# Later modulation products, four row buffers and GpSimd stores in a fused state-space and attention trunk

## The chip, the cores and the metric

The kernel runs on one core of a Trainium2 chip. A core has five engines that run side by side, each in the order of its own queue: TensorE (PE, matmuls), VectorE (DVE), ScalarE (ACT), GpSimd (POOL) and SyncE (SP, which here only issues transfers). Transfers (DMAs) between the chip's memory and the on-chip SBUF are issued from the queues of SP, ACT and POOL. The metric is the device time of one execution in microseconds, lower is better; a time is the median of several runs.

## The reference, cut to what matters

Two layers work on x, 1024 tokens of 1024 channels. Every sub-layer is modulated by a vector c:

```python
m = silu(c) @ w + b                     # shift, scale, gate: 64 columns of 128 in all
h = rms(x, g) * (1 + scale) + shift

# layer 0: state-space mixer
u, z = split(h @ w_in)
y = gelu(scan(u) + D * u)
y = y * sigmoid(y @ w_glu + b_glu)      # "GLU"
y = y * silu(z)
x = x + gate * (y @ w_out)              # "output projection"

# shared keys, values, forget gates; layer 1: attention with decay
h = rms(x, kv_g) * (1 + scale) + shift
k, v, f = split(h @ kv_w)               # k with a norm per head
h = rms(x, b_g) * (1 + scale) + shift
q, z = split(h @ w_in)                  # q with a norm per head
o = attention(q, k, v, cumsum(log_sigmoid(f)))
x = x + gate * ((o * silu(z)) @ w_out)
```

The modulation `silu(c) @ w` has 64 outputs per partition. Each needs one tile of 128 x 1024 weights (512 KB) and one dot product of its rows with silu(c).

## The kernel before, in words

x is kept transposed, channels on partitions, in eight strips of 128 channels by 1024 tokens. Every matmul that must be precise is made of three: both operands are split into a high and a low half (`split`, lines 99 to 101; `split_part`, line 705) and the three larger products are added in PSUM.

The work runs in stages: preparation and the in-projection, the scan with the rest of the in-projection, the GLU (lines 742 to 762), the output projection (lines 773 to 804), the norm for the shared keys and values (lines 818 to 825), six token-wise jobs called v0, v2, k0, k2, q0 and q2 (lines 918 to 952), attention with the z strips of layer 1 between its steps, and the last projection.

The instructions are not run in the order in which the code gives them. A planner simulates the five engines and, on each, takes what is ready by then, earlier code first; a transfer or an instruction whose inputs are expected early can be drawn far ahead of its place. `tc.issue_after(i)` only says that what is issued in its block stays behind instruction `i` on that engine. On the chip each engine then runs its list strictly in order, and waits at an instruction whose inputs are not there.

Modulation: 16 of the 64 rows (shift and scale of layer 0) are handled at the start. `modulate(n0, n1)` (lines 135 to 139) treats the other 48: a buffer of the pool `mwp`, which has two, a load from SP's queue, and `gemv` (line 131), one DVE instruction that multiplies by silu(c) and sums. The GLU calls it for three rows in each of five slots (line 755), the output projection for one row in nine slots (line 784), the token jobs for two rows at twelve places in v0, v2 and k0 (line 941).

A GLU slot (e, i) is one strip e of output channels and one half i of the tokens. It loads z (line 750, two buffers) and, at i = 0, y (line 752); scales z (line 756), takes its sigmoid (line 757) and forms silu (line 758); projects (line 759), takes the sigmoid of the result (line 760), and multiplies both into y (lines 761 and 762). The first two projections, `psg`, are made before the slots begin. Projections have two PSUM buffers (`pj`).

An output slot (e, i) loads x (line 780), projects (line 785), adds the gated result to x (`L786`), stores the new x row to `x1_d` (line 788) for the last stage, and squares it (line 790). GpSimd adds the squares up (line 794); two matmuls with a constant matrix (lines 800 and 801) turn the sum into the mean square over all channels, and `neg2_rsqrt` into the inverse root. The new x is then scaled in place by it, strips in turn on DVE and GpSimd (line 824), and `modulated` makes the split operands `aH` and `aL` of the token jobs (lines 165 to 167).

A token job takes 2 x 256 columns of weights (`wide`, line 829, one raw buffer of 1 MB) and makes sixteen tiles of 128 tokens by 256 columns (`token_tile`, three PSUM buffers). A V tile is split (lines 862 and 863, `vt`, two buffers) and stored (line 866). A K or Q tile has a norm per head (lines 874 to 879: square on ACT, sum on DVE, two small steps on GpSimd, product `hnt` on DVE), four of them are turned on PE and stored (line 894).

At job q0 the pools of x1 and of modulation are closed, and the attention's tiles (`at0`) take over their memory as its last readers finish.

## Time and profile before

| | |
|---|---|
| Median of 3 runs | 1225.57 us (1224.21 to 1227.58) |
| The profiled execution's own time | 1223.69 us |
| Its span, first to last instruction | 1221.9 us |
| Mean granted TensorE clock | 0.987 |
| PE busy | 1162.0 us, 95% of the span |
| DVE, ACT, POOL busy | 848.9, 605.1, 367.8 us |
| GLU and output projection | about 299 to 495 us |
| Token jobs | about 487 to 820 us |
| Attention and last stage | about 820 to 1222 us |

In a row of a group or a timeline, `L132` is line 132 of the kernel, `out<-in` are tile names, and what stands in brackets is the idle time of the engine before the instruction and what ended it. `SPq` and `POOLq` are the issuing queues. A row of waits gives who waited for whom, the time in all, how often and the longest. Times within the span count from its start.

### The profile page before, as it was taken

The numbers are of one execution on the slowest core, as the hardware profiler recorded it, in microseconds if no ns is written. First come the engines' busy times: TensorE is split into PE (matmuls) and PEld (weight loads), VectorE is DVE, ScalarE is ACT, GpSimd is POOL, SyncE is SP. The second block draws the span as 40 slices with busy tenths as digits, with TensorE's granted clock in tenths as the row PEclk, the third lists the DMA queues.
The fourth block names the chain that finished last, engine by engine and source line by source line (L and its number), as shares of the span: only waits on it lengthen the run. The fifth ranks groups of instructions, "written<-read, shape, count | busy, mean of one in ns | idle before, by whom it ended". The sixth has DMA issues, their size and how long they took to land.

```text
span 1221.9 us, 20599 instructions
## 1 busy us (share of the span) xinstructions
PE 1162.0 (95%) x7542; PEld 1017.3 (83%) x7542; DVE 848.9 (69%) x1724; ACT 605.1 (50%) x1138; POOL 367.8 (30%) x568
## 2 busy tenths in 40 slices
PE   8989898997899998899989999999999999999898
PEld 6778887887778876799989989998888888888686
DVE  7889899874498767746444664448787778887421
ACT  6565766665335324322213452227677777886310
POOL 4000000000000033600133463447576666764100
PEclk9999999998989999999999999999999999999999
DMA  9754666584974885247543277518796968871242
GB/s 352 220 173 117 171 169 164 154 233 126 334 249 129 281 312 167 90 154 233 200 148 139 83 214 152 156 70 182 132 188 124 171 122 155 156 138 27 94 165 78
DMA packets 113333, 205.30 MB, mean 168 GB/s; under 512 B 17072, under 2 KB 58160, under 8 KB 111696
## 3 DMA queue, kind: packets, MB, share of 16 engines
q1 hardware_dynamic: 86272, 161.44, 41.4%
q0 software_dynamic: 24960, 37.75, 18.1%
q10 hardware_dynamic: 2000, 4.79, 1.7%
q8 instruction: 60, 0.98, 0.3%
q14 instruction: 41, 0.34, 0.1%
HBM read 146.47 MB, written 46.20 MB: 158 GB/s over the span
## 4 chain that ended last, share of the span: by engine, by line
PE 57%; DVE 16%; DMA 12%; ACT 5%; issue 5%; SPq 2%; POOL 2%; ACTq 0%; POOLq 0%; DVEq 0%
PE tkps L851 16%; PE zb L112 7%; PE pj_f L112 5%; PE tp L1043 5%; DMA modw<-modw 4%; PE u L264 4%; PE ov L1049 3%; PE ov L1050 3%; PE sp L1010 3%; DMA v_d<-vt 3%; PE sp L1011 3%; PE pj_g L112 2%; DMA mwx<-modw 2%; PE f L112 2%; DVE w_lo L101 1%
## 5 line engine op out<-in xcount | busy, mean ns | idle before, releaser
L851 PE MATMUL tkps<-wvh,aH 128*128 128x256 f32 (+1 forms) x768 | 220.5, 287 | 7.3 <-DVE vt L863 4.0
L851 PE MATMUL tkps<-wvh,aL 128*128 128x256 f32 (+1 forms) x768 | 217.1, 283 | 1.4 <-DVE aL L167 1.4
L851 PE MATMUL tkps<-wvl,aH 128*128 128x256 f32 (+1 forms) x768 | 216.7, 282 | 0.0
L851 PEld LDWEIGHTS tkps<-wvh,aH 128*128 128x128 f32 x768 | 145.2, 189 | 9.8 <-DVE vt L863 4.9
L851 PEld LDWEIGHTS tkps<-wvh,aL 128*128 128x128 f32 x768 | 145.1, 189 | 2.1 <-DVE aL L167 1.8
L851 PEld LDWEIGHTS tkps<-wvl,aH 128*128 128x128 f32 x768 | 145.3, 189 | 0.3 <-issue 0.2
L1045 ACT ACTIVATE pth<-tp 128x512 fp32r<-128x512 f32 (+1 forms) x192 | 87.2, 489 | 61.4 <-PE ov L1049 34.7
L1018 ACT ACTIVATE pr<-pr,mx 128x128 f32<-128x128 f32 (+7 forms) x128 | 98.9, 773 | 22.4 <-DVE mx L1015 21.8
L1020 POOL TENSOR_SCALAR pr<-pr,sm 128x128 f32<-128x128 f32 (+7 forms) x128 | 96.2, 761 | 40.6 <-DVE sm L1019 40.5
L1046 DVE TENSOR_TENSOR ptl<-tp,pth 128x512 fp32r<-128x512 f32 (+1 forms) x192 | 101.3, 551 | 9.0 <-ACT pth L1045 8.6
L93 ACT ACTIVATE w_hi<-w_raw 128x1024 fp32r<-128x1024 f32 x49 | 51.6, 1053 | 86.4 <-PE pj_f L112 29.5
L1015 DVE CUSTOM_DVE_ANT_0 pr<-sp,fb 128x512 f32<-128x512 f32 (+3 forms) x128 | 72.8, 569 | 21.3 <-PE tp L1043 19.9
L1049 PE MATMUL ov<-pth,vhl 128*128 128x256 f32 x320 | 85.6, 299 | 0.1
L1043 PE MATMUL tp<-ident,pr 128*128 128x128 f32 x576 | 82.9, 273 | 0.0
L874 ACT ACTIVATE hsq<-tkps 128x256 f32<-128x256 f32 x64 | 24.6, 384 | 117.8 <-PE tkps L851 112.5
L132 DVE CUSTOM_DVE_ANT_0 modw<-modw,c_b 128x1024 f32<-128x1024 f32 x48 | 58.6, 1223 | 34.0 <-DMA modw<-modw 33.7
L1050 PE MATMUL ov<-ptl,vhl 128*128 128x256 f32 x320 | 81.0, 286 | 0.2 <-DVE ptl L1046 0.2
L1010 PE MATMUL sp<-kk,qs 128*128 128x256 f32 (+2 forms) x192 | 74.5, 388 | 2.2 <-DVE mx L1015 1.9
L1043 PEld LDWEIGHTS tp<-ident,pr 128*128 128x128 f32 x576 | 65.3, 140 | 7.1 <-POOL pr L1020 0.5
L794 POOL TENSOR_TENSOR sq<-sq,sq 128x512 f32<-128x512 f32 x12 | 19.0, 1585 | 173.3 <-ACT sq L790 173.3
L877 POOL TENSOR_TENSOR hms<-hms,nhalf 128x4 f32<-128x4 f32 x64 | 67.6, 1057 | 5.0
L876 POOL TENSOR_SCALAR hms<-hms 128x4 f32<-128x4 f32 x64 | 15.2, 237 | 176.3 <-DVE hms L875 172.4
(325 smaller groups left out, 3305.4 us busy)
## 6 DMA issues: line engine op xcount, KB each, us to landing
modw<-modw SPq DMA_DIRECT2D x48, 512.0 KB, 5.1
kk<-k_d POOLq DMA_DIRECT2D x32, 512.0 KB, 6.8
wvr<-kvq_w SPq DMA_DIRECT2D x12, 1024.0 KB, 5.5
mwx<-modw SPq DMA_DIRECT2D x16, 512.0 KB, 7.5
w_raw<-a_w_in SPq DMA_DIRECT2D x16, 512.0 KB, 5.2
v_d<-vt SPq DMA_DIRECT2D x32, 256.0 KB, 2.5
fb<-f_d SPq DMA_DIRECT2D x16, 512.0 KB, 8.9
vhl<-v_d POOLq DMA_DIRECT2D x16, 512.0 KB, 9.7
```

What stands on the lines that cost most here:

```text
L112: T.matmul(ps, w[wt][:, k, :], act[at][k][half], start=(k == k0 and n == 0), stop=(k == k1 and n == 2))
L851: T.matmul(ps[:, 0:nv], at, wt[:, k, 0:nv], start=(n == 0), stop=(n == 3 * KT - 1))
L877: G.tensor_tensor(out=ms, in0=ms, in1=nhalf, op=ALU.pow)
L1010: T.matmul(sp[:, 0:wm_], qsl, kk[:, 0, lo:lo + wm_], start=True, stop=False)
L1015: V.tensor_tensor_reduce(out=pr[:, lo:hi], in0=sp[:, 0:w_], in1=fb[:, lo:hi], scale=1.0, scalar=3e38 if m0 is None else m0, op0=ALU.add, o ...
L1018: S.activation(pr[:, 0:nk], pr[:, 0:nk], AF.Exp, scale=-1.0, bias=mx, accum_out=sm)
L1020: G.tensor_scalar(out=pr[:, 0:nk], in0=pr[:, 0:nk], scalar1=sm, scalar2=0.0, op0=ALU.mult, op1=ALU.add)
L1043: T.transpose(out=tp[:, b, :], in_=prs[qi][:, P * (b0 + b):P * (b0 + b) + P], identity=ident)
L1045: S.activation(pth[:, 0:m, dst], tp[:, 0:m, :], AF.Copy)
L1046: V.tensor_tensor(out=ptl[:, 0:m, dst], in0=tp[:, 0:m, :], in1=pth[:, 0:m, dst].bitcast(F32), op=ALU.subtract)
L1049: T.matmul(ov, vhl[:, b, :], pth[:, b - b0, :], start=(b == 0), stop=False)
L1050: end = T.matmul(ov, vhl[:, b, :], ptl[:, b - b0, :], start=False, stop=(b == nb - 1)).ins
```

## The change: what it does

- `modulate` becomes two helpers. `mod_load` allocates a buffer and issues one row's load behind a given transfer on SP. `mod_take` issues the products of the rows held beyond a number `keep`, behind a given DVE instruction.
- Each of the 16 GLU slots and 16 output slots now loads one row, and takes the product of the row loaded two slots before, behind the slot's last DVE instruction. Jobs v0 and v2 load one row at every second tile, sixteen in all, and keep one row back; of the remaining products one runs in k0 and the last is placed behind the last head norm of k2.
- The pool of rows has four buffers in place of two (16 KB a partition for 8), and GpSimd's DMA descriptor memory is set to 8192 bytes in the call that makes the program; before it had the default, twice that.
- The new x rows are stored from GpSimd's queue in place of SP's.
- For e = 0 the sigmoid of the projection is issued first, and the sigmoid of z in every slot behind it.

```diff
@@ -35,7 +35,6 @@
 MAGIC = 12582912.0
 LOOK = 2
 U_FIRST = 4
-GLU_MOD = 5
 F_ROWS, Z_END = 2, 2
 Z_FIRST, Z_STEP = 8, 2
 ORDER = ((0, 0), (0, 1), (0, 2), (0, 3), (1, 0), (1, 1), (1, 2), (1, 3))
@@ -132,11 +131,22 @@
             V.tensor_tensor_reduce(out=mw, in0=mw, in1=c_b, scale=1.0, scalar=0.0,
                                    op0=ALU.mult, op1=ALU.add, accum_out=mod[:, n:n + 1])
 
-        def modulate(n0, n1):
-            for n in range(n0, n1):
+        mod_next, mod_held = [2 * KT], []
+
+        def mod_load(behind):
+            n = mod_next[0]
+            if n < 64:
                 mw = mwp.tile([P, D], F32, name="modw", tag="modw")
-                Q.dma_start(out=mw, in_=a["modw"][n])
-                gemv(mw, n)
+                with tc.issue_after(behind):
+                    Q.dma_start(out=mw, in_=a["modw"][n])
+                mod_held.append((n, mw))
+                mod_next[0] += 1
+
+        def mod_take(behind, keep=0):
+            while len(mod_held) > keep:
+                n, mw = mod_held.pop(0)
+                with tc.issue_after(behind):
+                    gemv(mw, n)
 
         def mod_bias(lo, hi, nm):
             t = ctile([P, hi - lo], nm)
@@ -725,7 +735,7 @@
 
 
         x1_d = dram.tile([D, L], F32, name="x1_d", tag="x1_d")
-        mwp = modx.enter_context(tc.tile_pool(name="mwp", bufs=2, side="right", reuse_waits="tile"))
+        mwp = modx.enter_context(tc.tile_pool(name="mwp", bufs=4, side="right", reuse_waits="tile"))
         lx = ExitStack()
         xnp = lx.enter_context(tc.tile_pool(name="xnp", bufs=1, side="right", reuse_waits="tile"))
         x1 = [xnp.tile([P, L], F32, name=f"x1_{k}", tag=f"x1_{k}") for k in range(KT)]
@@ -747,19 +757,22 @@
                 zs = wk.tile([P, HL], F32, name="zs", tag="zs")
                 sg = wk.tile([P, HL], F32, name="sg", tag="sg")
                 with tc.issue_after(last_y):
-                    Q.dma_start(out=zt, in_=z_d[P * e:P * e + P, i])
+                    last_q = Q.dma_start(out=zt, in_=z_d[P * e:P * e + P, i]).ins
                     if i == 0:
-                        yd[e] = Q.dma_start(out=yt[e], in_=y_rows(e)).ins
-                    elif e < GLU_MOD:
-                        with tc.issue_after(yd[e]):
-                            modulate(16 + 3 * e, 19 + 3 * e)
+                        last_q = Q.dma_start(out=yt[e], in_=y_rows(e)).ins
+                mod_load(last_q)
                 V.tensor_tensor(out=jk(zt), in0=jk(zt), in1=q2p[:, i], op=ALU.mult)
-                S.activation(zs, zt, AF.Sigmoid, bias=biz[:, e:e + 1])
+                if e == 0:
+                    sg_end = S.activation(sg, psg[i], AF.Sigmoid, bias=vec["b_glu"][:, 0:1]).ins
+                with tc.issue_after(sg_end):
+                    S.activation(zs, zt, AF.Sigmoid, bias=biz[:, e:e + 1])
                 V.scalar_tensor_tensor(out=zs, in0=zt, scalar=biz[:, e:e + 1], in1=zs, op0=ALU.add, op1=ALU.mult)
-                ps = project(wg[e], act, i, f"g{e}_{i}") if e else psg[i]
-                S.activation(sg, ps, AF.Sigmoid, bias=vec["b_glu"][:, e:e + 1])
+                if e:
+                    ps = project(wg[e], act, i, f"g{e}_{i}")
+                    S.activation(sg, ps, AF.Sigmoid, bias=vec["b_glu"][:, e:e + 1])
                 V.tensor_tensor(out=zs, in0=sg, in1=zs, op=ALU.mult)
-                V.tensor_tensor(out=part(yt[e], i), in0=part(yt[e], i), in1=jk(zs), op=ALU.mult)
+                gated = V.tensor_tensor(out=part(yt[e], i), in0=part(yt[e], i), in1=jk(zs), op=ALU.mult).ins
+                mod_take(gated, 2)
             act = act_tiles()
             for i in range(2):
                 for k in range(KT):
@@ -778,14 +791,11 @@
                     held[e] = (len(seen) + sum(seen), weight_strip(a["a_w_out"][e], [P, KT, P], V, wk))
                 xr = wk.tile([P, HL], F32, name="xr", tag="zt2")
                 xd = Q.dma_start(out=xr, in_=a["xT"][:, e, sl]).ins
-                n = 16 + 3 * GLU_MOD + sum(seen) - 1
-                if sum(seen) and n < 40:
-                    with tc.issue_after(xd):
-                        modulate(n, n + 1)
+                mod_load(xd)
                 ps = project(held[e][1], act, i, f"o{e}_{i}")
-                V.scalar_tensor_tensor(out=kj(x1[e][:, sl]), in0=jk(ps), scalar=gate_a[:, e:e + 1], in1=kj(xr),
-                                       op0=ALU.mult, op1=ALU.add)
-                Q.dma_start(out=x1_d[P * e:P * e + P, sl], in_=x1[e][:, sl])
+                mod_take(V.scalar_tensor_tensor(out=kj(x1[e][:, sl]), in0=jk(ps), scalar=gate_a[:, e:e + 1], in1=kj(xr),
+                                                op0=ALU.mult, op1=ALU.add).ins, 2)
+                G.dma_start(out=x1_d[P * e:P * e + P, sl], in_=x1[e][:, sl])
                 sq = wk.tile([P, HL], F32, name="sq1", tag="sg" if seen[i] else "zs" if i else "acc", bufs=1 if seen[i] == 0 and i == 0 else 2)
                 sq_end = S.activation(sq, x1[e][:, sl], AF.Square).ins
                 if seen[i] == 0:
@@ -860,10 +870,11 @@
                 vt = wv.tile([P, 4, 2, HD], F32R, name="vt", tag="vt")
                 pv = ps[:, 0:256].rearrange("p (h d) -> p h d", d=HD)
                 S.activation(vt[:, :, 0, :], pv, AF.Copy)
-                V.tensor_tensor(out=vt[:, :, 1, :], in0=pv, in1=vt[:, :, 0, :].bitcast(F32), op=ALU.subtract)
+                vl = V.tensor_tensor(out=vt[:, :, 1, :], in0=pv, in1=vt[:, :, 0, :].bitcast(F32), op=ALU.subtract).ins
                 if qd == 0:
                     V.tensor_copy(out=flog[:, t, :], in_=ps[:, 256:nv])
                 Q.dma_start(out=v_d[P * t:P * t + P, 4 * qd:4 * qd + 4, :], in_=vt.rearrange("p h a d -> p h (a d)").bitcast(F32))
+                return vl
 
 
             def qk_tile(w, t):
@@ -918,6 +929,7 @@
             for j, job in enumerate(("v0", "v2", "k0", "k2", "q0", "q2")):
                 kind, n0 = job[0], int(job[1])
                 if job == "q0":
+                    mod_take(last_nt[-1])
                     s_b = mod_scale(48, 56, vec["b_g"], "s_b")
                     sh_b = mod_bias(40, 48, "sh_b")
                     gate_b = mod_bias(56, 64, "gate_b")
@@ -936,14 +948,17 @@
                 ws = [wide(src[base + n0 + d], a["kv_wf"] if job == "v0" and d == 0 else None) for d in range(2)]
                 for i in range(2):
                     for d in range(2):
-                        if j < 3:
-                            with tc.issue_after(wide_dma[-1]):
-                                modulate(40 + 8 * j + 4 * i + 2 * d, 42 + 8 * j + 4 * i + 2 * d)
-                        if kind == "v":
-                            for t in range(4 * i, 4 * i + 4):
-                                v_tile(n0 + d, ws[d], t)
-                        else:
-                            nts = [qk_tile(ws[d], t) for t in range(4 * i, 4 * i + 4)]
+                        nts = []
+                        for t in range(4 * i, 4 * i + 4):
+                            if kind == "v":
+                                end = v_tile(n0 + d, ws[d], t)
+                            else:
+                                nts.append(qk_tile(ws[d], t))
+                                end = last_nt[-1]
+                            if t % 2:
+                                mod_take(end, 1)
+                                mod_load(wide_dma[-1])
+                        if kind != "v":
                             gain = vec["kg"] if kind == "k" else qgm
                             qk_half(nts, gain, 2 * (n0 + d), i, k_d if kind == "k" else q_d)
                 if job == "v0":
@@ -1207,7 +1222,7 @@
     import concourse.bacc as bacc
 
     arrays = pack(inputs)
-    nc = bacc.Bacc("TRN2", target_bir_lowering=False, num_devices=1)
+    nc = bacc.Bacc("TRN2", target_bir_lowering=False, num_devices=1, dynamic_dma_scratch_size=8192)
     aps = {k: nc.dram_tensor(k, v.shape, mybir.dt.from_np(v.dtype), kind="ExternalInput").ap() for k, v in arrays.items()}
     out = nc.dram_tensor("out_0_dram", (D, L), F32, kind="ExternalOutput").ap()
     with tile.TileContext(nc, schedule_with_timeline_sim=True) as tc:
```

## The prediction

> **What bounds the kernel now.** I read the page's head first, then busy time by stretch.
>
> ```profile
> span 1221.9 us, 20599 instructions
> PE 1162.0 (95%) x7542; PEld 1017.3 (83%) x7542; DVE 848.9 (69%) x1724; ACT 605.1 (50%) x1138; POOL 367.8 (30%) x568
> ```
>
> The profiled execution took 1223.69 us around its span of 1221.9; the median of the timed runs is 1225.57. My sum is made against 1223.69 and its difference is then taken from the median, which is 1.88 longer. TensorE (PE) is busy 95% of the span, so an edit is worth only the PE idle time, or lowered clock, that it removes or adds. The columns below are the stretch, its length, busy time of PE, weight loads, VectorE (DVE), ScalarE (ACT) and GpSimd (POOL), granted clock, DMA share and GB/s.
>
> ```profile
> 320.00:360.00 40.00, 36.50 (x146) 28.99 (x145) 28.19 (x44) 11.16 (x15) 0.00 (x0) 0.91 0.93 288
> 360.00:440.00 80.00, 80.00 (x345) 64.23 (x344) 65.43 (x92) 33.80 (x48) 5.87 (x5) 1.00 0.67 225
> 460.00:480.00 20.00, 17.70 (x64) 12.21 (x63) 13.95 (x20) 5.75 (x8) 2.85 (x2) 0.91 0.68 217
> 480.00:500.00 20.00, 16.84 (x83) 13.53 (x82) 19.86 (x18) 9.25 (x12) 17.03 (x9) 1.00 0.22 67
> 526.00:592.00 66.00, 63.53 (x518) 63.00 (x517) 29.51 (x54) 17.38 (x31) 1.28 (x1) 0.97 0.55 185
> 592.00:626.00 34.00, 28.85 (x239) 28.05 (x239) 18.51 (x35) 6.70 (x13) 8.16 (x10) 1.00 0.71 232
> 626.00:660.00 34.00, 34.00 (x291) 34.00 (x292) 16.46 (x31) 10.08 (x18) 14.42 (x24) 1.00 0.32 114
> ```
>
> In most of the GLU and the output projection (360 to 440) PE never stops. It stops early in the GLU (3.50 us in 320 to 360, with the clock at 0.91), late in the output projection (2.30 in 460 to 480, again 0.91), in the norm that follows it (3.16 in 480 to 500, where DVE is busy 19.86 of 20), in the V job (2.47 in 526 to 592) and in the first K job (5.15 in 592 to 626). From 626 on it is full. Next, what the modulation products do to DVE, and where they run (columns: stretch, length, DVE busy with their number, clock, DMA share, GB/s):
>
> ```profile
> DVE modw L132 <- DMA modw<-modw: 33.7, 23, 4.6
> ```
> ```profile
> 300.00:399.00 99.00, 18.29 (x15) 0.97 0.71 223
> 399.00:475.00 76.00, 20.90 (x17) 0.98 0.87 295
> 475.00:526.00 51.00, 0.00 (x0) 1.00 0.26 83
> 526.00:592.00 66.00, 9.58 (x8) 0.97 0.55 185
> 592.00:626.00 34.00, 9.78 (x8) 1.00 0.71 232
> ```
>
> 48 products of (18.29 + 20.90 + 9.58 + 9.78)/48 = 1.22 us, and 33.7 us in which DVE, an in-order queue, stood at a product whose row was not there. Most of that is beside full PE. Eight products that the code puts into the first V job were drawn ahead, so 17 run in the output projection and none from 475 to 526. PE's own waits, by stretch, say which stand-stills count:
>
> ```profile
> PE ms L800 <- POOL sq L794: 2.1, 1, 2.1
> PE pj_o L112 <- DVE w_lo L101: 0.5, 1, 0.5
> ```
> ```profile
> PE tkps L851 <- DVE hnt L879: 2.1, 2, 1.6
> PE trps L886 <- DVE hnt L879: 1.9, 1, 1.9
> PE tkps L851 <- DVE vt L863: 1.1, 1, 1.1
> ```
>
> **First gain: the output projection's end.** Rows of the timeline, one engine after another:
>
> ```profile
> 459.23 1.22 DVE L132 CUSTOM_DVE_ANT_0 modw<-modw,c_b 128x1024 f32<-128x1024 f32 x1 [1.51 <-DMA modw<-modw]
> ...
> 461.77 1.30 DVE L786 SCALAR_TENSOR_TENSOR x<-pj_o,gate_a,xr 128x512 f32<-128x512 f32 x1
> ...
> 463.94 1.26 POOL L794 TENSOR_TENSOR sq<-sq,sq 128x512 f32<-128x512 f32 x1 [5.06 <-ACT sq L790]
> ...
> 465.25 2.01 PE L800 MATMUL ms<-sq,onesm 128*128 128x512 f32 x2 [2.08 <-POOL sq L794]
> ```
>
> A product waits 1.51 us for its row, another follows, and only then does the residual of a finished projection run (L786, 461.77). Its square and GpSimd's sum (463.94) follow, and PE waits 2.08 for them at the mean square (L800). With products two slots behind their loads, a product issued behind a residual finds its row there, so this wait should go whole, with the 0.5 at L112 (the lower weight half, also behind a product). The clock was 0.91 over these 20 us: 0.09 x 20 = 1.8 more. Gain 0.5 + 2.1 + 1.8 = **4.4**; if the dip came from elsewhere, 2.6.
>
> **Second gain: the K job.** The eight products there go: with one load in each of 32 slots and 16 in the two V jobs, all 48 rows are loaded before it, and only two products are left for it and later. The three waits above are 2.1 + 1.9 + 1.1 = 5.1, and the longest stands behind this row:
>
> ```profile
> 616.10 1.23 DVE L132 CUSTOM_DVE_ANT_0 modw<-modw,c_b 128x1024 f32<-128x1024 f32 x1 [3.01 <-DMA modw<-modw]
> ```
>
> 3.01 us of DVE waiting for a row, with the head norms (hnt) queued behind. The stretch after it, the same work without products, has PE at 34.00 of 34. I leave 0.5 for the remaining product and the stores' buffers: gain **4.6**, bounds 2 (the waits on hnt halve) and 5.1.
>
> **First cost: products pushed into the norm.** With products tied one to a slot, numbers 42 to 45 follow the last four residuals (474 to 502) and 46 and 47 the first V tiles, where before none ran: 6 x 1.22 = 7.3 us on the DVE that is full from 480 to 500, ahead of the norm's own work since the code comes earlier. The first falls into the wait for the mean square. What else can hide is DVE's idle time there:
>
> ```profile
> 506.23 0.42 DVE L863 TENSOR_TENSOR vt<-tkps,vt 128x256 fp32r<-128x256 f32 x1 [3.21 <-ACT vt L862]
> ...
> 512.29 0.42 DVE L863 TENSOR_TENSOR vt<-tkps,vt 128x256 fp32r<-128x256 f32 x1 [3.04 <-ACT vt L862]
> ```
>
> 3.21 and 3.04 us, room for two or three. So two to three are exposed, and PE, which waits for DVE in this stretch already, passes them on: 2.5 x 1.22 = **3.1** lost, bounds 0 (all fall in gaps) and 7.3. The four extra products of the V jobs beyond that cost nothing: DVE is busy 29.51 of 66 there.
>
> **Second cost: x rows stored by GpSimd.** 16 stores leave SP and go to POOL. SP's issue, and the nearest store from POOL's queue, twice the bytes over the same 128 partitions:
>
> ```profile
> L788 SPq DMA_DIRECT2D x_d<-x x16: 326/327/327, 403.4 to 502.6; - x16
> ```
> ```profile
> L632 POOL DMA_DIRECT2D y_d<-r x8: 531/532/783, 132.6 to 289.0; - x8
> ```
>
> SP loses 16 x 0.33 = 5.2 us of issuing, and xr and modulation loads no longer queue behind a store that waits for a residual; PE gains from that only what is counted above. POOL gains 16 x 0.53 = 8.5 us; twelve stores lie where POOL is nearly idle, four in the norm, where it is busy 17.03 of 20: 2.1 us, of which I count **0.5**, bounds 0 and 2.1. [...] The eight stores of y above, issued while DVE was busy too, spread from 0.531 to 0.783 us only, a delay of 0.25, so I make no case of it.
>
> **GLU.** Silu behind the first sigmoids frees a PSUM buffer earlier, but PE does not wait for that one. It waits here:
>
> ```profile
> 315.10 9.59 SPq L752 DMA_DIRECT2D yt<-y_d  x5
> 324.79 1.74 SPq L750 DMA_DIRECT2D zt<-z_d  x1
> ...
> 331.11 0.69 DVE L756 TENSOR_TENSOR zt<-zt,q2p 128x512 f32<-128x512 f32 x1 [7.30 <-DMA zt<-z_d]
> 332.39 1.23 DVE L132 CUSTOM_DVE_ANT_0 modw<-modw,c_b 128x1024 f32<-128x1024 f32 x1 [0.59 <-DMA modw<-modw]
> ...
> 335.61 0.69 ACT L760 ACTIVATE sg<-pj_g,vecs 128x512 f32<-128x512 f32 x1
> ...
> 336.35 0.79 PE L112 MATMUL pj_g<-aH,w_hi 128*128 128x512 f32 x1 [3.50 <-ACT sg L760]
> ```
>
> The third z load (324.79) stands on SP behind five y loads that take 9.59 us to issue and moves data behind theirs, so zt is 7.30 late; then a product and its wait (332.39 to 333.61) delay the chain zt, zs, the product with sg, the next sg, and PE by 1.2. The change removes that 1.2, but now three rows rather than two may load ahead of that z load: 0.52 MB at the 288 GB/s of this stretch is 1.8. Net loss **0.6**. Bounds: a gain of 3.5 + 0.09 x 40 = 7.1 if the z load gets ahead of the y loads; a loss of 3.6 if it falls behind two more rows.
>
> **The rest.** Eight loads move into the first V job, where stores of V went unhindered, against later, where rows loaded between them:
>
> ```profile
> v_d<-vt SPq DMA_DIRECT2D x12, 256.0 KB, 2.4
> ```
> ```profile
> v_d<-vt SPq DMA_DIRECT2D x20, 256.0 KB, 3.6
> ```
>
> 2.4 us to land against 3.6. A V tile takes PE 63.53/518 x 24 matmuls = 2.9 and has two buffers, so 3.6 still fits into 5.7: 0.3, bounds 0 and 2.5 (what the V stretch lost). The last product now stands behind the second K job's last norm, near 720, and the attention's first tiles take over its memory; the first of them is written here:
>
> ```profile
> 716.75 0.60 ACT L991 ACTIVATE o_t<-zb 128x512 f32<-128x512 f32 x1
> ```
>
> Three us later is nothing to PE unless ACT stands in front of its squares: 0.3, bounds 0 and 3. The halved descriptor memory of GpSimd's queue: no row shows it full, so 0; no row bounds it either, short of those of the y stores (0.78 for 0.53).
>
> Sum: -4.4 - 4.6 + 3.1 + 0.5 + 0.6 + 0.3 + 0.3 = -4.2. Profiled 1223.69 - 4.2 = 1219.5; median 1225.57 - 4.2 = **1221.4**.
>
> **Rivals.** (1) *The norm takes it all back*: every one of the six products passes to PE, 7.3 instead of 3.1, net 0.0: 1225.6. For it: 19.86 of 20 on DVE. Against: the gaps of 3.21 and 3.04. (2) *Slower, by GpSimd's queue.* Today POOL's share of the scaling and DVE's late residual run like this:
>
> ```profile
> 480.49 6.92 POOL L824 TENSOR_TENSOR x<-x,q2x 128x512 f32<-128x512 f32 x4 [2.08 <-DVE q2x L159]
> ```
> ```profile
> 486.17 1.22 DVE L786 SCALAR_TENSOR_TENSOR x<-pj_o,gate_a,xr 128x512 f32<-128x512 f32 x1
> ```
>
> If the store of that residual (ready at 487.39) is put on POOL before the four scalings that start at 480.49, POOL stands 6.9 us at it, the scaled rows are late and the norm grows by about 6.9 for one half: -4.2 + 6.9 = +2.7; with rival 1's products +6.9, so 1228 to 1232. It decides as soon as the planner expects the residual before the inverse root. Against: the planner placed POOL's sum of the same rows after the scalings. (3) *The GLU's stall goes as well*: -4.2 - 0.6 - 7.1 = -11.9: 1213.7. For it: the chain there is a chain of late loads; against: z's load hangs on y's, which nobody moves. (4) *The change doesn't do what it says*: products are again drawn ahead or bunched, PE's waits stay: 1225.6.
>
> **Numbers.** A measurement tells about 0.3%, 3.7 us, from no change. Forecast 0.48 (own range 1217.5 to 1224.5: 0.32 of it faster, 0.16 within); rival 1 0.25 (0.20 within, 0.05 slower); rival 2 0.12, slower; rival 3 0.13, faster; rival 4 0.02, within. So faster 0.45, same 0.38, slower 0.17. The range reaches from rival 3's edge, 1214, to the middle of rival 2, 1230, and leaves out some 0.2.
>
> **What would show it.** Right: no DVE idle put down to modw loads; no product between 592 and about 700 but one or two; PE full there; no wait at L800. Costs: products between the last residuals and the V tiles, PE waits on aL and on L112's lower half longer than 3.16 together; POOL idle waiting for x ahead of L824 speaks for rival 2. The forecast is wrong if the K job's waits stay, or if the GLU's 3.50 changes by more than 2.

## The result, and the profile after

The changed kernel takes 1211.97 us (median of 4 runs, 1210.69 to 1212.2) against 1225.34 for the kernel before (4 runs, 1224.21 to 1227.58): ratio 0.9887, 95% interval 0.9869 to 0.9904. The forecast was 1221.4 with 1214 to 1230: the measured time lies below the range, and the gain is three times the one forecast. (A ratio here is worked out from all runs of both kernels and isn't quite that of the two medians.) The profiled execution took 1212.13 us, 11.56 less than the one before; the sum had said 4.2 less.

The head of the page after, and the same stretches as before in the view by stretch (stretch, length, busy time of PE, weight loads, DVE, ACT, POOL, granted clock, DMA share, GB/s):

```profile
span 1210.4 us, 20601 instructions
PE 1160.9 (96%) x7542; PEld 1019.5 (84%) x7542; DVE 854.3 (71%) x1724; ACT 605.7 (50%) x1138; POOL 376.9 (31%) x584
```
```profile
320.00:360.00 40.00, 37.21 (x160) 29.54 (x159) 29.47 (x44) 13.82 (x20) 0.00 (x0) 1.00 0.88 269
360.00:440.00 80.00, 78.91 (x340) 63.43 (x339) 71.71 (x99) 32.52 (x46) 15.25 (x14) 1.00 0.74 253
460.00:480.00 20.00, 19.40 (x82) 14.63 (x80) 14.23 (x14) 10.00 (x13) 8.09 (x7) 1.00 0.37 116
480.00:500.00 20.00, 15.72 (x82) 13.00 (x82) 18.96 (x25) 8.00 (x12) 13.09 (x10) 0.91 0.48 159
526.00:592.00 66.00, 64.26 (x534) 63.36 (x533) 34.32 (x61) 16.80 (x30) 1.94 (x1) 1.00 0.70 224
592.00:626.00 34.00, 34.00 (x292) 34.00 (x291) 16.28 (x32) 9.14 (x18) 12.06 (x20) 1.00 0.30 110
```

PE's busy time is nearly what it was (1160.9 for 1162.0): most of what went is idle time, and in the stages below a part is lowered clock. The clock is 1.00 in the GLU (320 to 360) and the V job (526 to 592), where it had been 0.91 and 0.97, and the K job is full from 592 on, where PE had stood 5.15. The bad stretch is now 480 to 500, with PE at 15.72 of 20 and the clock at 0.91; there, where the kernel before had 1.00, the clock stood at half for 3.4 us:

```profile
484.48:487.87 3.39, 2.86 (x7) 2.29 (x8) 3.39 (x5) 0.63 (x1) 2.07 (x2) 0.50 0.44 149
```

Such a stretch at half clock is called a dip below; it costs 0.50 x 3.4 = 1.7 us.

What VectorE waited for, in the view of the row tile (a line for each cause would stand under the second line):

```profile
L131 DVE CUSTOM_DVE_ANT_0 modw<-modw,c_b x48: 1203/1215/1254, 335.1 to 706.8; 128x1024 f32<-128x1024 f32 x48
its engine sat idle before it (us, times) until:
who waited for it (us, times):
```

All 48 products find their row there: none of the 33.7 us of waits is left. PE's own waits, in the GLU and in the V job:

```profile
PE pj_g L111 <- ACT sg L772: 2.8, 1, 2.8
```
```profile
PE tkps L861 <- DVE vt L873: 1.2, 2, 0.9
```

The GLU's stall is still there, 2.8 for 3.5. Around the last projections, the waits of the kernel before (460 to 515) and of the changed one (455 to 510):

```profile
PE ms L800 <- POOL sq L794: 2.1, 1, 2.1
PE ms L801 <- ACT sq L790: 1.8, 1, 1.8
...
PE pj_o L112 <- DVE w_lo L101: 1.3, 1, 1.3
PE pj_o L112 <- DVE x L786: 0.5, 1, 0.5
```
```profile
PE pj_o L111 <- DVE w_lo L100: 3.0, 1, 3.0
PE pj_o L111 <- DVE x L796: 1.8, 2, 1.5
PE tkps L861 <- DVE flog L875: 1.6, 1, 1.6
```

The two at the mean square (2.1 and 1.8) are gone; those at the projections grew from 1.3 and 0.5 to 3.0 and 1.8, and a first token tile waits 1.6 where it had waited 1.4 for `aL`. That is where six products now run (columns: stretch, length, busy time of the products with their number, clock, DMA share, GB/s):

```profile
468.00:515.00 47.00, 7.35 (x6) 0.96 0.41 135
533.00:592.00 59.00, 12.15 (x10) 1.00 0.74 233
592.00:620.00 28.00, 2.43 (x2) 1.00 0.27 95
620.00:646.00 26.00, 0.00 (x0) 1.00 0.36 125
```

To say which stage gained, I cut each profiled execution at starts of matmuls in its trace: GLU from the first GLU projection to the end of the last; then to the first token tile (output projection); then 288 matmuls of token tiles (norm), the next 480 (V), the next 384 (K), and the rest. In us, with the median of the timed runs and the ratio to the kernel before. The runs were timed in several sessions, in which the kernel before had medians of 1223.11 to 1226.26, so the ratio, which is to the kernel before of the same session, compares better than the median:

| kernel | GLU | output | norm | V | K | median | ratio, 95% |
|---|---|---|---|---|---|---|---|
| before | 95.99 | 90.87 | 51.25 | 61.84 | 54.40 | | |
| after | 92.68 | 87.59 | 54.41 | 58.89 | 48.28 | 1211.97 | 0.9887 (0.9869 to 0.9904) |
| e1 silu only | 92.84 | 91.53 | 51.11 | 63.39 | 54.46 | 1225.50 | 1.0005 (0.9986 to 1.0024) |
| e2 four buffers only | 96.16 | 94.16 | 50.77 | 62.08 | 51.33 | 1221.55 | 0.9973 (0.9957 to 0.9990) |
| e3 no lag | 92.59 | 86.59 | 54.79 | 59.12 | 48.36 | 1212.46 | 0.9899 (0.9873 to 0.9925) |
| e4 x rows on SP | 92.74 | 87.57 | 56.93 | 57.26 | 48.28 | 1212.24 | 0.9904 (0.9879 to 0.9929) |
| e5 silu undone | 93.97 | 87.60 | 54.91 | 57.18 | 48.27 | 1211.55 | 0.9889 (0.9862 to 0.9915) |
| e6 four slots freed | 92.41 | 87.58 | 52.68 | 58.63 | 48.26 | 1209.42 | 0.9884 (0.9851 to 0.9917) |
| e7 V rows in pairs | 92.12 | 87.58 | 54.93 | 63.84 | 50.52 | 1218.26 | 0.9940 (0.9916 to 0.9965) |
| e8 K rows back in pairs | 93.72 | 87.58 | 53.82 | 57.40 | 55.87 | 1225.00 | 0.9996 (0.9975 to 1.0017) |
| e9 z before y | 89.45 | 89.00 | 54.98 | 57.19 | 48.27 | 1208.77 | 0.9864 (0.9834 to 0.9893) |
| e10 six slots freed | 93.24 | 87.60 | 52.39 | 58.26 | 50.03 | 1210.99 | 0.9886 (0.9854 to 0.9918) |
| e11 e9 and e10 | 89.45 | 88.80 | 52.54 | 58.12 | 49.78 | 1209.42 | 0.9865 (0.9835 to 0.9896) |
| e12 K rows back, single | 92.79 | 87.60 | 53.77 | 59.31 | 48.46 | 1212.38 | 0.9903 (0.9871 to 0.9935) |
| e13 two buffers, no lag | 93.09 | 86.25 | 54.73 | 57.36 | 48.32 | 1209.19 | 0.9875 (0.9848 to 0.9902) |
| e14 e9 and e6 | 89.76 | 89.31 | 52.39 | 57.38 | 48.26 | 1212.43 | 0.9894 (0.9869 to 0.9920) |

From before to after: GLU -3.3, output -3.3, norm +3.2, V -3.0, K -6.1; what lies ahead -0.5, the rest +1.5 (with a dip near 761). The stages of one execution scatter by a microsecond or two (norm and V trade: 54.41 and 58.89 after, 56.93 and 57.26 in e4), so a verdict below rests on a stage only where it moved by more, or where rows show why.

### The profile page after: what moved, and what is told of

Its sections match the earlier page's. It is cut to its first block, busy times and chain, and to the rows that moved or that the text cites. A ratio compares the mean times of both kernels' runs of the same rounds, so it can differ in the third digit from the quotient of the medians.

```text
span 1210.4 us, 20601 instructions
## 1 busy us (share of the span) xinstructions
PE 1160.9 (96%) x7542; PEld 1019.5 (84%) x7542; DVE 854.3 (71%) x1724; ACT 605.7 (50%) x1138; POOL 376.9 (31%) x584
## 4 chain that ended last, share of the span: by engine, by line
PE 68%; DVE 12%; DMA 8%; ACT 5%; issue 4%; POOL 2%; SPq 1%; ACTq 0%; POOLq 0%; DVEq 0%
PE tkps L861 17%; PE zb L111 7%; PE pj_o L111 6%; PE pj_f L111 5%; PE tp L1058 5%; PE pj_g L111 5%; PE u L274 4%; PE ov L1064 3%; PE ov L1065 3%; PE sp L1025 3%; PE sp L1026 3%; DMA v_d<-vt 2%; PE f L111 2%; PE z L274 2%; DVE w_lo L100 1%
## 5 line engine op out<-in xcount | busy, mean ns | idle before, releaser
L1025 PE MATMUL sp<-kk,qs 128*128 128x256 f32 (+2 forms) x192 | 74.5, 388 | 2.4 <-DVE mx L1030 1.9
L890 DVE TENSOR_TENSOR hnt<-tkps,hms 128x256 f32<-128x256 f32 x64 | 27.0, 422 | 59.3 <-POOL hms L888 59.2
L1026 PE MATMUL sp<-kk,qs 128*128 128x256 f32 (+2 forms) x192 | 65.6, 342 | 0.0
L100 DVE TENSOR_TENSOR w_lo<-w_raw,w_hi 128x1024 fp32r<-128x1024 f32 x39 | 54.2, 1390 | 15.6 <-ACT w_hi L92 15.1
```

Of the source, the lines that this page charges most:

```text
L1025: T.matmul(sp[:, 0:wm_], qsl, kk[:, 0, lo:lo + wm_], start=True, stop=False)
L1026: T.matmul(sp[:, 0:wm_], qsl, kk[:, 1, lo:lo + wm_], start=False, stop=not last)
```

## Experiments: which part of the change does it

**e1, silu alone.** The kernel before with only the new order of the sigmoids.

```diff
+                if e == 0:
+                    sg_end = S.activation(sg, psg[i], AF.Sigmoid, bias=vec["b_glu"][:, 0:1]).ins
+                with tc.issue_after(sg_end):
+                    S.activation(zs, zt, AF.Sigmoid, bias=biz[:, e:e + 1])
```

> The kernel before with one edit: the sigmoids of the two early projections are issued first and the silu sigmoids behind them. Theory: in both profiles the silu sigmoid of the first slot starts within 0.2 us of the same time and PE waits for a z row, not for these sigmoids, so this edit is worth nothing: within 2 us of before, PE's wait for sg stays 3.5 (+-0.5). Rival (the edit freed the GLU's chain): PE's wait falls to about 2.8, the clock between 320 and 360 goes to 1.00 and 3 to 4 us are gained.

Ratio 1.0005: nothing. Yet its GLU is 3.2 shorter than before. PE's wait there, VectorE's waits for rows, and the stretch with the clock:

```profile
PE pj_g L112 <- ACT sg L764: 3.1, 1, 3.1
```
```profile
DVE modw L132 <- DMA modw<-modw: 30.7, 25, 4.0
```
```profile
320.00:360.00 40.00, 36.87 (x159) 29.51 (x158) 30.58 (x48) 13.53 (x18) 0.00 (x0) 1.00 0.96 302
```

Stall 3.1 for 3.5, clock 1.00 where the kernel before showed 0.91 (0.09 x 40 = 3.6). So some 3 us of GLU can come and go with the clock, under the same rows and nearly the same waits.

**e5, silu undone.** The changed kernel with the old order.

```diff
-                if e == 0:
-                    sg_end = S.activation(sg, psg[i], AF.Sigmoid, bias=vec["b_glu"][:, 0:1]).ins
-                with tc.issue_after(sg_end):
-                    S.activation(zs, zt, AF.Sigmoid, bias=biz[:, e:e + 1])
+                S.activation(zs, zt, AF.Sigmoid, bias=biz[:, e:e + 1])
```

> The changed kernel with the old order of silu (sigmoid of z first, sigmoid of the projection behind it); rows, places, buffers and stores as changed. The GLU, from its first projection to its last, took 92.6 to 92.8 us in every kernel with the new order (the changed kernel, silu alone, no lag, x rows on SP) and 96.0 to 96.2 in the two with the old one. If the order of silu gave the GLU's 3.3 us, this kernel's GLU is back at 96 and the time near 1215. If the rows and their places gave it, or the clock of the moment, the GLU stays at 92.6 to 93 and the time at 1212.

1211.55, as changed: the order of silu gives nothing here either. Its GLU is 93.97; the ten microseconds with the stall and the wait:

```profile
330.00:340.00 10.00, 7.31 (x25) 5.50 (x24) 8.91 (x14) 3.89 (x6) 0.00 (x0) 0.83 0.84 286
```
```profile
PE pj_g L111 <- ACT sg L768: 2.7, 1, 2.7
```

A stall of 2.7 and a dip to 0.83; the changed kernel had 2.8 and no dip. The 1.3 between the two GLUs is about the dip (0.17 x 10 = 1.7).

**e4, x rows stored by SP.** The changed kernel with the stores back on SP.

```diff
-                G.dma_start(out=x1_d[P * e:P * e + P, sl], in_=x1[e][:, sl])
+                Q.dma_start(out=x1_d[P * e:P * e + P, sl], in_=x1[e][:, sl])
```

> The changed kernel with the x rows stored from SP's queue again. Theory: with rows two slots ahead it no longer matters that a load stands behind a store on SP, and GpSimd loses 16 x 0.56 us of issuing, of which only the four in the norm touch anything: within 2 us of the changed kernel, norm at most 1 us shorter. Rival (the stores held up the loads): DVE waits for rows return in the output projection and the time is 3 us or more above the changed kernel.

1212.24: the move is worth nothing. What the stores cost on GpSimd, and how long they took to land, in the changed kernel and in e4:

```profile
L798 POOL DMA_DIRECT2D x_d<-x x16: 539/557/582, 400.2 to 495.8; - x16
```
```profile
x_d<-x POOLq DMA_DIRECT2D x16, 256.0 KB, 4.2
```
```profile
x_d<-x SPq DMA_DIRECT2D x16, 256.0 KB, 3.1
```

0.54 to 0.58 us each, with VectorE busy 76.79 of the 96 us from 400 to 496, landing after 4.2 us for 3.1 from SP: the issue stays under 0.6, and the median landing grew by 1.1.

**e2, four buffers alone.** The kernel before with four row buffers and the halved descriptor memory.

```diff
-        mwp = modx.enter_context(tc.tile_pool(name="mwp", bufs=2, side="right", reuse_waits="tile"))
+        mwp = modx.enter_context(tc.tile_pool(name="mwp", bufs=4, side="right", reuse_waits="tile"))
-    nc = bacc.Bacc("TRN2", target_bir_lowering=False, num_devices=1)
+    nc = bacc.Bacc("TRN2", target_bir_lowering=False, num_devices=1, dynamic_dma_scratch_size=8192)
```

> The kernel before with four row buffers and the smaller descriptor memory, everything else as it was: three rows in every other GLU slot, products right behind their loads, products still in the first K job. Theory (what matters is where products and loads stand): loads run two rows further ahead, so DVE's 33.7 us of waiting for rows falls to 10 to 20, but the K job keeps eight products and the V job its pairs of loads: gain 2 to 5 us. Rival (buffers are the whole of it): DVE waits under 5 us and 10 us or more are gained. If the halved descriptor memory costs anything, the attention stage gets longer than before by more than 1 us.

```profile
DVE modw L132 <- DMA modw<-modw: 16.1, 10, 5.7
```

Half of VectorE's waits for rows go (16.1 for 33.7), and 3.7 of the 13 us (1225.25 to 1221.55). The K stage gets 3.1. What lies behind the K stage, the attention among it, took 567.44 for 568.37, so no cost of the smaller descriptor memory shows.

**e3, no lag.** The changed kernel with each product in the slot of its own load.

```diff
-                mod_take(gated, 2)
+                mod_take(gated)
...
-                            if t % 2:
-                                mod_take(end, 1)
-                                mod_load(wide_dma[-1])
+                            if t % 2:
+                                mod_load(wide_dma[-1])
+                                mod_take(end)
```

> The changed kernel with the lag taken away: each row's product behind the same slot's (or tile's) last DVE work, four buffers and all places of loads kept. Theory (lag): products meet rows still on their way, DVE waits 15 us or more for rows in all and the time is 4 to 8 us above the changed kernel. Rival (places and buffers alone do it): with 11 us between slots and loads issued at the slot's start the rows are there, DVE waits under 5 us, and the time is within 2 us of the changed kernel.

1212.46. VectorE waits for a row once:

```profile
DVE modw L131 <- DMA modw<-modw: 0.4, 1, 0.4
```

My theory, that the lag is what brings the rows in time, falls.

**e13, two buffers as well.** e3 with `bufs=2`: the new places and nothing else that could hold a row.

```diff
-        mwp = modx.enter_context(tc.tile_pool(name="mwp", bufs=4, side="right", reuse_waits="tile"))
+        mwp = modx.enter_context(tc.tile_pool(name="mwp", bufs=2, side="right", reuse_waits="tile"))
```

> The changed kernel with two row buffers and, since two do not allow it, no lag: each slot's row is multiplied behind the slot's last instruction. If the places (one row a slot, one every second tile) are what took the waits away, VectorE's waits for rows stay under 3 us (33.7 before, 0.4 with four buffers and no lag), the V and K stages stay at 58 to 59 and 48.3, and the time at 1212. If the buffers are needed, the waits return to 10 or more, K is at 50 or above, and the time at 1216 to 1220.

```profile
DVE modw L131 <- DMA modw<-modw: 1.3, 2, 1.1
```

1209.19, with 1.3 us of waits for rows and a K stage of 48.32. Neither the lag nor the two further buffers is needed: one row to a slot, its load at the slot's start and its product behind the slot's last instruction, has the whole gain.

## Experiments: where in the kernel

**e8, rows back in the K job.** Eight of the sixteen late rows in k0, in pairs at the start of each four tiles.

```diff
                         nts = []
+                        if j == 2:
+                            for _ in range(2):
+                                mod_load(wide_dma[-1])
+                                n, mw = mod_held.pop()
+                                gemv(mw, n)
...
-                            if t % 2:
+                            if t % 4 == 3 and j < 2:
```

> The changed kernel with eight of the sixteen late rows put back into job k0, in pairs, loaded and multiplied at the start of each four tiles as before; v0 and v2 load one row behind every fourth tile instead of every second. Four buffers. If the products in the K job themselves cost its 6.1 us (54.40 to 48.28), the K stage is back at 54 and the time near 1218. If what cost there was mostly the wait for rows with two buffers, the K stage is where four buffers alone put it, at 51.3 (so 3.1 longer than in the changed kernel), and the time near 1215. If eight products cost nothing once their rows are in time, it stays at 48.3 and 1212.

1225.0, the whole gain gone. VectorE's waits for rows, and PE's waits from 500 to 830:

```profile
DVE modw L131 <- DMA modw<-modw: 6.1, 5, 2.2
```
```profile
PE trps L897 <- DVE hnt L890: 7.4, 3, 4.3
PE tkps L861 <- ACT aH L175: 4.2, 1, 4.2
PE tkps L861 <- DVE hnt L890: 2.9, 3, 1.6
```

The K stage is 55.87, more than before, with 6.1 us of waits for rows. Of the waits shown, 3.2 of the 7.4 and 2.0 of the 2.9 lie in the K stage, with a dip of the clock near 620. The other 8 us lie behind it, and look like an accident of this edit: it kept two earlier rows for q0, whose operands need them. Their products run at 699.13 and 700.27; PE waits 4.3 for a head norm at 699.27, at the end of k2, and q0's first tile 4.2 for `aH`. So e8 prices the K stage (7.6) and not the whole.

**e12, the same rows, single.** Eight rows in k0 again, one at every second tile, and none but the last kept.

```diff
-                            if t % 2:
+                            if t % (2 if j == 2 else 4) == 1 and j < 3:
```

> The changed kernel with eight of the sixteen late rows put into job k0 as in the run that put them back in pairs, but one at every second tile, with one row held back as in the V jobs; v0 and v2 load one row at every fourth tile, and only the last row is left for q0. The pairs gave a K stage of 55.87. If the eight products themselves cost that (1.2 us each ahead of the head norms), the K stage is 53 to 56 here too and the time 1218 or more. If the waits for their rows cost it (five products in that stage, spread, had cost nothing when the last output slots were freed), it is 48.3 to 49 and the time 1212 or, with fewer loads beside the stores of V, a little less.

1212.38. The K stage in two stretches, and the products that fall into it:

```profile
592.00:620.00 28.00, 28.00 (x240) 27.96 (x240) 15.20 (x31) 7.02 (x14) 10.60 (x16) 1.00 0.55 189
620.00:640.00 20.00, 20.00 (x172) 19.94 (x171) 13.47 (x26) 6.53 (x12) 7.61 (x14) 1.00 0.61 195
```
```profile
L131 DVE CUSTOM_DVE_ANT_0 modw<-modw,c_b x7: 1215/1217/1218, 601.6 to 637.9; 128x1024 f32<-128x1024 f32 x7
```

PE is full, with seven products in the stage, and the stage is 0.2 longer than with two. Placed singly, the products in the K job cost next to nothing. What cost in e8 came with placing them in pairs right behind their loads, waits for rows among it; the pairs and the waits aren't told apart.

**e7, V rows in pairs.**

```diff
-                            if t % 2:
-                                mod_take(end, 1)
-                                mod_load(wide_dma[-1])
+                            if t % 4 == 3:
+                                mod_take(end)
+                                mod_load(wide_dma[-1])
+                                mod_load(wide_dma[-1])
```

> The changed kernel with the rows of v0 and v2 loaded in pairs behind every fourth tile, and their products taken there in pairs, in place of one at every second tile; their number is the same. If single loads gave the V stage's 2.9 us (61.84 to 58.89: stores of V no longer behind two rows), the stage is back at 61 to 62 and the time near 1215. If the V stage gained only because fewer rows are left for it or because of the clock, it stays near 59 and the time at 1212.

1218.26. The V stage is 63.84, longer than before; the changed kernel's and this one's, and what ACT waited for there:

```profile
533.35:592.24 58.89, 57.72 (x486) 57.24 (x485) 29.52 (x51) 14.68 (x26) 0.00 (x0) 1.00 0.74 234
```
```profile
532.02:595.86 63.84, 59.98 (x486) 58.88 (x485) 29.11 (x51) 14.90 (x26) 0.00 (x0) 0.97 0.68 221
```
```profile
ACT vt L872 <- DMA v_d<-vt: 28.8, 10, 6.9
```
```profile
ACT vt L872 <- DMA v_d<-vt: 45.4, 16, 9.5
```

The same number of products; ACT waits 45.4 us for stores of V to land and free `vt`, against 28.8, and PE idles 3.86 for 1.17 with the clock at 0.97. So two rows loaded side by side hold up the stores more than single rows do. PE's longest wait there, 2.40 at 549.73, goes back over VectorE to a `vt` for which ScalarE stood 9.54 for a store. The K stage, with four products in it and no wait for a row, is 2.2 longer too.

The kernel before had its main stall in another way. ScalarE's waits for stores in its V stage (537 to 599) were shorter than the 28.8 above, and PE stood behind products on VectorE, the second of which waited for its row:

```profile
ACT vt L862 <- DMA v_d<-vt: 20.2, 7, 5.9
```
```profile
552.20 1.23 DVE L132 CUSTOM_DVE_ANT_0 modw<-modw,c_b 128x1024 f32<-128x1024 f32 x1 [1.56 <-DMA modw<-modw]
...
557.22 0.39 PE L851 MATMUL tkps<-wvh,aH 128*128 128x256 f32 x1 [2.11 <-DVE vt L863]
```

VectorE ran one product at 549.41, waited 1.56, ran the next, then split a weight (2.29), and only at 556.76 the V tile that PE needed. e1 shows both ways at the old places: 2.21 at 553.33 behind such a pair, and 1.79 at 561.03 behind a store. In e2, where no row is late in this stage, the V stage is still 62.08, and its stall of 2.07 at 564.94 goes back to a store.

**e6 and e10, last output slots freed.** The changed kernel without rows in the last four (e6) or six (e10) output slots; they move on to v0, v2 and k0.

```diff
-                mod_load(xd)
+                if sum(seen) < 12:      # e10: 10
+                    mod_load(xd)
...
-                mod_take(V.scalar_tensor_tensor(...).ins, 2)
+                res = V.scalar_tensor_tensor(...).ins
+                if sum(seen) < 12:
+                    mod_take(res, 2)
```

> The changed kernel without the loads and products in the last four output slots; the four rows move on into the jobs v0 to k0, at the same one for every two tiles. If the products pushed into the norm cost the 3.1 us that this stage grew by (51.25 to 54.41), the norm falls to 51.3 to 52 and, as the K job now has five products instead of one but each with its row loaded four buffers ahead, the time falls to 1209 to 1210. If the norm's growth comes from something else (the code of the norm starts earlier, and waits for the same things), the norm stays near 54.4 and the time at 1212.

> The changed kernel without loads and products in the last six output slots; they move on into v0 to k0, one for every two tiles. With four slots free the norm fell from 54.41 to 52.68, with two products left in it; the kernel before had 51.25 and none. If each product there costs its share, the norm falls to 51.3 and the time to 1209; K has seven products, each with its row in time, and stays at 48.3. If the last 1.4 us of the norm are from elsewhere, it stays near 52.7 and the time near 1209.5.

The products left between 468 and 515 in e6:

```profile
468.00:515.00 47.00, 2.42 (x2) 1.00 0.30 97
```

Two in place of six, and the norm falls by 1.7 to 2.0; 1.1 to 1.4 of its growth stays with two left. The clock goes with the products: e6 from 480 to 500,

```profile
480.00:500.00 20.00, 16.71 (x93) 13.32 (x94) 15.73 (x17) 7.63 (x12) 14.90 (x11) 1.00 0.24 80
```

is at 1.00, as are the other three kernels with freed slots (e10, e11, e14) and the three with the old places (before, e1, e2). All nine with a row in every output slot show 0.83 or 0.91 there. In the whole norm stage PE idles 51.25 - 44.69 = 6.6 us before, 54.41 - 46.61 = 7.8 after and 52.68 - 45.93 = 6.75 in e6; the one dip of the changed kernel costs 1.7 more. So the six products came with some 1.2 us of waiting and a dip, together nearly the whole growth of 3.2, and freed slots take both away but for 0.2. The stage falls by less than the two make together, since PE is busy longer at full clock (45.93 for 44.69); why isn't shown. The medians, 1209.42 and 1210.99, are not told from the changed kernel's.

In e10 the K stage is 1.75 longer, with eight products in it and no wait for a row; six in e6 cost nothing and seven in e12 cost 0.2. It isn't the eighth product. The stage begins late, since ScalarE waits for a store of V at its start; in e10, and the same place in e6:

```profile
594.57 0.38 ACT L875 ACTIVATE vt<-tkps 128x256 fp32r<-128x256 f32 x1 [7.48 <-DMA v_d<-vt]
```
```profile
590.14 0.89 ACT L875 ACTIVATE vt<-tkps 128x256 fp32r<-128x256 f32 x2 [5.31 <-PE tkps L864]
```

PE's two waits in the stage, 0.28 at 595.46 and 0.76 at 602.14, come right behind it; from there on PE stands for nothing, with seven of the eight products still to come. Why that store is late in e10 isn't known.

**e9, z before y.** Each strip's y load behind the z load of its own slot.

```diff
-                        last_q = Q.dma_start(out=yt[e], in_=y_rows(e)).ins
+                        with tc.issue_after(last_q):
+                            last_q = Q.dma_start(out=yt[e], in_=y_rows(e)).ins
```

> The changed kernel with each strip's y load put behind the z load of its own slot on SP (the third z load stood behind four y loads that took 8.16 us to issue; now two of weights stand ahead of it instead). If the late z load is what makes PE stand in the GLU (2.2 to 2.8 us in every kernel with the changed rows, 3.1 to 3.5 before), the stall falls below 1, the GLU from 92.7 to 90 or less and the time to 1209. If the wait is for the buffer of z or the chain behind it, whatever SP does, the stall stays at 2.2 to 2.8 and the time at 1212. If the y loads are late in their turn, DVE waits for yt and the GLU is longer than 92.7.

SP's queue and VectorE at the third z load in the changed kernel, then SP in e9, and e9's GLU:

```profile
315.64 8.16 SPq L762 DMA_DIRECT2D yt<-y_d  x4
323.90 1.68 SPq L760 DMA_DIRECT2D zt<-z_d  x1
...
330.67 0.69 DVE L764 TENSOR_TENSOR zt<-zt,q2p 128x512 f32<-128x512 f32 x1 [6.07 <-DMA zt<-z_d]
```
```profile
307.91 0.33 SPq L760 DMA_DIRECT2D zt<-z_d  x1
```
```profile
320.00:360.00 40.00, 40.00 (x174) 32.31 (x173) 31.38 (x48) 12.32 (x17) 0.00 (x0) 1.00 0.78 243
```

The third z load goes out at 307.91 in place of 323.90, and PE never stops from 320 to 360: the late load behind the y loads was the cause of the GLU's stall in the changed kernel. The kernel before shows the same rows, but no run moved its y loads. The GLU is 3.2 shorter, the seam behind it 1.4 longer, and the median 1208.77.

**e11 and e14, the two together.** e9 with e10's edit, and with e6's.

> Both edits: y loads behind the slot's own z load, and the last six output slots without rows. If the two are independent, their gains add: 1212 less 3 for the GLU and less 3 for the norm, 1206. If the z load is not the cause of the GLU's stall, 1209.

> The changed kernel with y loads behind the slot's own z load, and without rows in the last four output slots (with six freed slots beside it the K stage was 49.8, with eight products in it; with four freed slots alone it was 48.3, with six). If both gains stand and K is free again: GLU 89.4, norm 52.6, K 48.3 and the time 1206. If K stays at 49.8: 1208.

1209.42 and 1212.43: the gains do not show in the medians as a sum. In the profiled execution of e14 (1209.81) the edited stages are where they were expected (89.76, 52.39, 48.26), but the part behind the token jobs, which no edit touches, took 404.98 for 401.97 us. A dip near 831 is 1.7 of that; for the rest the cause was not found. All of e6, e9, e11 and e13 have medians 2.5 to 3.2 under the changed kernel's, as much as the sessions differ, and intervals that overlap its own: none is shown to beat it.

## Why the prediction was wrong

In the profiled executions the gain is 7.4 us more than the sum said. The GLU gave 3.9 more than forecast, the V job 3.3, the K job 1.5 and the norm 0.4; the output projection gave 1.1 less and the rest 0.7 less. By the terms of the sum:

- **GLU, +0.6 forecast, -3.3 measured: mis-sized.** The working charged 1.8 for one more row ahead of the third z load and granted 1.2 for the product taken out of the chain. The row cost next to nothing: z came at 330.67 for 331.11, since SP now issues four y loads ahead of it (8.16 us) where it had issued five (9.59). The product did leave the chain (it runs at 335.06, behind the sigmoid that PE waits for), and the stall fell by 0.7. The other 2.6 went with the clock, whose dip was counted only at the lower end of the range, as if it came with the stall for sure. Rival 3 had the cause right (z's load hangs on y's), and e9 shows it; but the change did not remove it.
- **V job, +0.3 forecast, -3.0 measured: wrong in sign.** This step failed most plainly. Loads in the first V job were charged as a delay of the stores, from 2.4 to 3.6 us of landing. The second V job's stall, 2.47 us and the clock at 0.97, stood in the quoted row, and nothing was granted for parting its pairs or for taking away their waits. The rows before that stall are products: a pair on VectorE, one waiting 1.56 for its row, with the V tile behind them. In the changed kernel the stage idles 1.17 in place of 2.47 and has no dip (1.7). e7 puts pairs back and the stage is 4.9 longer, though there it is stores that PE stands behind.
- **K job, -4.6 forecast, -6.1 measured: place right, size and reason not.** The bound of 5.1 was PE's listed waits; the stage gave 1 more, and why isn't shown. "The eight products there go" was taken as the reason; e12 has seven in the stage for 0.2. The pairs and the waits had to go, not the products.
- **End of the output projection, -4.4 forecast, -3.3 for the stage.** The wait at the mean square and the dip went as worked out: 460 to 480 has PE at 19.40 of 20 and the clock at 1.00. But the waits at the projections, of which 0.5 was to go, grew (1.3 and 0.5 to 3.0 and 1.8), in part in this stage.
- **Norm and GpSimd's stores, +3.6 forecast, +3.2 measured: the size right, by luck.** Six products run between 468 and 515, as counted. But the term was two to three products passed on as waiting, 3.1, and PE's waiting in the stage grew by 1.2 only; 1.7 is a dip of the clock that the term didn't have. Undoing the stores gains nothing in e4, and e6 and e10 leave 1.1 to 1.4 that freeing slots didn't bring back.
- **Rival 2** did not happen: GpSimd's scalings start at 474.42 in the trace after, ahead of the late stores. Rival 4 is out.
- **The lag**, which the first gain's working gave as its reason ("a product issued behind a residual finds its row there"), is not needed: e3 and e13.

The two signs that were to show the forecast wrong (K's waits stay; the GLU's 3.50 changes by more than 2) both failed to appear, and it was wrong all the same: no sign had been set for the V job, and none for the clock in the GLU.

The clock's share can be estimated. From the first GLU projection on, the dips cost 6.8 us in the profiled execution before (3.4 in the GLU, 1.7 each in the output projection and the V job) and 3.4 in the one after (1.7 each in the norm and near 761), so 3.4 of 11.6 would be clock. Over the timed runs the mean granted clock was 0.9850 for the kernel before (57 runs beside e1 to e12), 0.9888 for the one after (4 runs) and 0.9875 to 0.9888 for e3, e4, e5 and e13, which hold the same places; 1225.2 x 0.9850 / 0.9888 is 1220.5 and with 0.9875 it is 1222.1, so an estimate from the runs is 3 to 5 of the 13.4 us. The rest is idle time taken away. That fewer stalls of PE make fewer dips fits the runs (e8, with its stalls back, has 0.9838 for 0.9850 before), but no run here separates the two.

## What to carry to other kernels

Where an in-order engine does small side jobs whose data come by DMA, give each slot one of them, load at its start and product at its end, before adding buffers or a lag: here two buffers and no lag did as well as four and a lag of two, and the same products in pairs made a stage 5 us longer (V) or 8 (K, with waits for rows). When a stall is listed for a stage, ask of every edit that reaches that stage whether it takes it away, and write down a gain as readily as a cost. When a short stall of PE comes with a dip of its clock, put both into the range, since among kernels with nearly the same stall the dip came in some and stayed away in others (in the GLU, with stalls of 2.2 to 3.5 us, in three of twelve).

## What the runs showed of the hardware

A dip of the clock, where the traces show one, is 3.4 us at half clock (0.50 from 484.48 to 487.87 in the changed kernel) or two or three times that (in the kernel before 6.8 us in the GLU and 10.2 at 277; 10.2 in e8 near 700). Whether one follows a single stall of PE isn't told by its length. With one stall in the GLU the clock fell to 0.78 to 0.83 over ten microseconds in three profiled executions (stalls of 3.5, 2.7 and 2.4 us: before, e5, e8) and stayed at 1.00 in nine others (2.2 to 3.1 us: after, e1, e3, e4, e6, e7, e10, e12, e13); each kernel was profiled once. e2 stalls there several times, up to 1.9 us, without a dip. What decides whether a dip follows isn't shown.

The kernel before took from 1218.6 to 1231.63 us over its 57 timed runs beside e1 to e12, at granted clocks from 0.979 to 0.990, on the whole with the longer times at the lower clocks (correlation -0.70).
